# Gate and convolution projections of a hybrid decoder block: pairs of column blocks by seven block products in place of eight, gates parked in device memory

## The chip, the cores and the metric

One Trainium2 chip, one core. The metric is the device time of one execution in microseconds (us). All data are float32. A core has five engines with instruction queues of their own: TensorE (PE; loading its stationary operand is shown apart as PEld), VectorE (DVE), ScalarE (ACT), GpSimd (POOL) and SyncE (SP), whose queue here issues nearly all DMA transfers. Each queue is worked off in its order; an instruction that waits for a semaphore holds up those behind it.

## The reference

```python
h = rms_norm(x, norm_mix_g)                       # x: 1024 tokens x 1024
q, k, v, c_b, c_c, c_u, g_a, g_b = split(h @ w_in)  # 512 x 6 columns, then 1024 x 2
branch_a = stick_breaking_attention(q, k, v) @ w_sb_branch       # (512 -> 1024)
branch_b = short_conv_mixer(c_b, c_c, c_u, conv_w) @ w_conv_branch
merged = sigmoid(g_a) * branch_a + sigmoid(g_b) * branch_b
x = x + merged @ w_out
x = x + hierarchical_moe(rms_norm(x, norm_ffn_g))  # 32 experts, 2 per token
```

`short_conv_mixer` is c_b times a causal convolution of length 3, channel by channel, of c_c * c_u.

## The kernel before, in words

Every product is made from split operands: a float32 value is a high part (an fp32r copy, made on ACT) and a low part (value minus high part, made on DVE), and a product is three matmuls: high by high, high by low, low by high. In the projections the normalised, transposed input stands in SBUF as `hH` and `hL` (128 partitions x 8 k-blocks x 1024 tokens), a block of 128 weight columns is the stationary operand, and 512 tokens stream through.

The program has four stages. First (lines up to 570, put in order by a planner with costs, `Order`) come the norm, the projections q, k, v, the attention, and convolution block 0. Second, the stage that is edited, comes a plain list of jobs. Third are the output projection, second norm and routing, and fourth the experts, whose weights stream from memory.

A job makes one block of 128 output columns for 1024 tokens. `job_load` (L601 to L615) issues one DMA for the weights into one of two buffers `br`, and splits them into a third of `WH` and `WL` (three slots), ACT for the high part and DVE for the low one. `job_mm` (L617) does the matmuls, 48 with eight k-blocks and 24 with four, into two of the eight PSUM banks, and calls a closure that takes the result. The load of job n+2 is written ahead of the matmuls of job n.

The list has nine convolution jobs (blocks 1 to 3: c_c, c_u, c_b), then for each of eight merge blocks the gate g_b, its convolution branch, the gate g_a and its attention branch (the last two blocks are interleaved). `post_gb` and `post_ga` take a gate's sigmoid on ACT straight from PSUM, `post_bb` and `post_ba` multiply the branch by it on DVE, and POOL (DVE for the last two blocks) adds the two. The branches have k = 512. At the stage's start the attention output `attF` is split into `aH` and `aL`. In the last four jobs the blocks of w_out are loaded and split too (`out_w`).

Nothing plans this stage: each engine's order is that in which the code is written.

Of the kernel before, what the change touches and what calls it, by code (L numbers as in the profile page):

```python
# [21 lines left out]
F32 = mybir.dt.float32  # L22
# [8 lines left out]
N = 1024  # L31
# [67 lines left out]
def tile_hybrid_block(  # L99
# [481 lines left out]

    hlp = pool("hlp")
    aH = hlp.tile([128, 4, N], F32R, name="aH")
    aL = hlp.tile([128, 4, N], F32R, name="aL")
    c3 = hlp.tile([128, 2, 3, N], F32R, name="c3")
    v0 = VT0.rearrange("p t h d -> p (t h d)")
    cH = [v0[:, 0:N]] + [c3[:, 0, b] for b in range(3)]
    cL = [v0[:, N:2 * N]] + [c3[:, 1, b] for b in range(3)]
# [38 lines left out]
    hLk = [hL[:, k] for k in range(8)]  # L627
    aHk = [aH[:, k] for k in range(4)]
    aLk = [aL[:, k] for k in range(4)]

    cp = pool("cp", bufs=2)
    cst = {}

    def conv_jobs(b):
        def post_c(ps):
            cst["cc"] = cp.tile([128, N], F32, name="cc")
            S.activation(cst["cc"], ps, AF.Copy)

# [655 lines left out]
```

## Time and profile before

| | |
|---|---|
| time, three runs | median 1198.27 us (1198.21 to 1198.88) |
| the profiled execution | 1195.5 us, span 1193.7 us, mean granted clock 0.979 |
| PE, PEld busy | 1118.3 us (94%), 968.8 us (81%) |
| DVE, ACT, POOL busy | 761.7 us (64%), 656.8 us (55%), 343.2 us (29%) |
| the edited stage | 350.6 to 709.8 us |

The span runs from the first to the last instruction. Busy shares are means over stages with different limits; the rows below give the stage by itself. Instructions on one engine overlap a little, so that a busy time divided by a count is more than the distance from one start to the next.

### The profile page before, as it was taken

The page shows a single profiled execution, that of the slowest core. Times are in us where ns is not written, and L with a number is a line of the kernel's source. Part 1 is how long each engine was busy: PE and PEld are TensorE (multiplying, and loading weights), DVE is VectorE, ACT ScalarE, POOL GpSimd, SP SyncE. Part 2 cuts the span into 40 slices and gives each one's busy share as a digit, 9 for nine tenths or more (in the row PEclk, how much of TensorE's full clock was granted, in tenths as well). Part 3 has the DMA queues.
Part 4 walks back from the last instruction along what each step waited for, and adds up shares of the span by engine and source line. Part 5 has one row for each costly group of instructions (what it writes and reads, how often), then busy time and mean ns, then how long its engine had stood idle before and what let it go on. Part 6 is the DMA issues. An engine that isn't in the chain of part 4 may idle for free. (4 is left out here: it accounts for less than half of the span.)

```text
span 1193.7 us, 18153 instructions
## 1 busy us (share of the span) xinstructions
PE 1118.3 (94%) x6529; PEld 968.8 (81%) x6529; DVE 761.7 (64%) x1317; ACT 656.8 (55%) x1204; POOL 343.2 (29%) x661
## 2 busy tenths in 40 slices
PE   6999898998999999999999999899799999988894
PEld 5988797997788888888888888788588899977783
DVE  5579989989885332333233163444599998977683
ACT  6486768777654223222222132222489999977683
POOL 4636466363000000000000004545353223222121
PEclk9999999999999999999999999999899999999997
DMA  6000101001011111111112156837799999999992
GB/s 223 27 27 15 40 2 40 15 27 37 1 33 56 53 36 45 54 53 36 53 46 60 36 167 262 321 112 253 220 337 310 315 309 312 301 312 316 308 325 51
DMA packets 98323, 165.57 MB, mean 139 GB/s; under 512 B 13084, under 2 KB 62264, under 8 KB 98232
## 3 DMA queue, kind: packets, MB, share of 16 engines
q1 hardware_dynamic: 89016, 147.59, 36.8%
q0 software_dynamic: 9216, 16.81, 6.3%
q8 instruction: 52, 0.85, 0.3%
q14 instruction: 39, 0.32, 0.1%
HBM read 150.72 MB, written 19.92 MB: 143 GB/s over the span
## 5 line engine op out<-in xcount | busy, mean ns | idle before, releaser
L124 PE MATMUL PS<-WH,xet 128*88 128x256 f32 x768 | 153.2, 287 | 4.6 <-ACT sg L1159 4.6
L124 PE MATMUL PS<-hH,WH 128*128 128x512 f32 x448 | 143.9, 394 | 1.1 <-DVE attF L478 1.1
L124 PE MATMUL PS<-hH,WL 128*128 128x512 f32 x448 | 142.0, 390 | 0.0
L124 PE MATMUL PS<-hL,WH 128*128 128x512 f32 x448 | 141.9, 389 | 0.0
L124 PEld LDWEIGHTS PS<-WH,xet 128*88 128x88 f32 x768 | 109.5, 157 | 8.1 <-ACT sg L1159 5.4
L124 PE MATMUL PS<-WL,xet 128*88 128x256 f32 x384 | 109.2, 284 | 1.3 <-DVE WL L1103 1.2
L421 DVE TENSOR_TENSOR_SCAN pt<-pt 128x128 f32<-128x128 f32 (+2 forms) x96 | 93.4, 1013 | 16.3 <-issue 12.8
L674 POOL TENSOR_TENSOR mg<-mg,sga 128x1024 f32<-128x1024 f32 x6 | 14.7, 2455 | 293.0 <-DVE sga L672 293.0
L124 PEld LDWEIGHTS PS<-hH,WL 128*128 128x128 f32 x448 | 84.1, 188 | 17.6
L124 PEld LDWEIGHTS PS<-hH,WH 128*128 128x128 f32 x448 | 84.1, 188 | 17.5 <-ACT WH L610 1.2
L124 PEld LDWEIGHTS PS<-hL,WH 128*128 128x128 f32 x448 | 84.2, 188 | 16.4
L124 PE MATMUL PS<-WH,hH 128*128 128x384 f32 x256 | 91.8, 359 | 4.7 <-ACT hH L268 2.6
L611 DVE SCALAR_TENSOR_TENSOR WL<-br,cols,WH 128x128 fp32r<-128x128 f32 x200 | 68.9, 410 | 29.3 <-ACT WH L610 29.3
L124 PE MATMUL PS<-WH,hL 128*128 128x384 f32 x256 | 87.2, 340 | 0.1
L124 PE MATMUL PS<-WL,hH 128*128 128x384 f32 x256 | 86.7, 339 | 0.0
L615 DVE TENSOR_TENSOR WL<-br,WH 128x512 fp32r<-128x512 f32 x16 | 11.1, 691 | 116.5 <-ACT WH L614 116.5
L610 ACT ACTIVATE WH<-br,cols 128x128 fp32r<-128x128 f32 x200 | 65.4, 392 | 35.6 <-PE PS L124 34.4
L1092 POOL DMA_INDIRECT xr<-h2d,idx x32 | 45.3, 1414 | 78.7 <-PE PS L1134 69.5
L124 PE MATMUL PS<-WH,act 128*88 128x512 f32 x192 | 66.4, 400 | 1.2 <-ACT act L1168 1.2
L124 PEld LDWEIGHTS PS<-WL,xet 128*88 128x88 f32 x384 | 60.4, 157 | 4.6 <-DVE WL L1103 2.2
L124 PE MATMUL PS<-ahl,vt 128*128 128x256 f32 x320 | 53.5, 297 | 11.3 <-DVE attF L478 10.7
L460 POOL CAST ahl<-zeros 128x256 fp32r<-128x256 f32 x32 | 29.6, 934 | 115.3 <-PE PS L124 106.8
(278 smaller groups left out, 2735.1 us busy)
## 6 DMA issues: line engine op xcount, KB each, us to landing
br<-in_w_in_dram SPq DMA_DIRECT2D x25, 512.0 KB
cha<-in_w_gate_e_dram SPq DMA_DIRECT2D x22, 512.0 KB
cha<-in_w_up_e_dram SPq DMA_DIRECT2D x20, 512.0 KB
cha<-in_w_down_e_dram SPq DMA_DIRECT2D x18, 512.0 KB
mg<-in_w_down_e_dram SPq DMA_DIRECT2D x17, 512.0 KB
mg<-in_w_gate_e_dram SPq DMA_DIRECT2D x15, 512.0 KB
mg<-in_w_up_e_dram SPq DMA_DIRECT2D x14, 512.0 KB
br<-in_w_in_dram SPq DMA_DIRECT2D x36, 192.0 KB
```

The lines of the kernel that those rows point to most:

```text
L124: T.matmul(o, a, b, start=start, stop=stop)
L421: V.tensor_tensor_scan(pr, pr, pr, 1.0 if diag else P[:, j, w:w + 1], op0=OP.mult, op1=OP.bypass)
L460: G.tensor_copy(AHL[x][:, :, 0:128], zeros[:, None, :].to_broadcast([128, 2, 128]))
L610: S.activation(j.wH[:, k], r[:, k], AF.Copy, scale=g1[:, k:k + 1])
L611: V.scalar_tensor_tensor(j.wL[:, k], r[:, k], g1[:, k:k + 1], j.wH[:, k], op0=OP.mult, op1=OP.subtract)
L615: V.tensor_sub(j.wL[:, 0:nk], r[:, 0:nk], j.wH[:, 0:nk])
L674: (G if b < 6 else V).tensor_add(mg, mg, mst[b].rearrange("p (t c) -> p t c", c=128))
L1092: G.indirect_dma_start(out=XE[e % 2][:, :], out_offset=None, in_=h2d[:, :], in_offset=bass.IndirectOffsetOnAxis(ap=idx[0:SLOTS, EX[e]:EX[e ...
```

## The change

Two column blocks that are read from the same h make a pair. With K halved (k-blocks 0 to 3 and 4 to 7) and the tokens halved, a pair is a 2 x 2 by 2 x 2 block product, and it is made from seven block products of sums (a Strassen-Winograd scheme) in place of eight. There are eleven pairs: (c_c, c_u) of convolution blocks 2 and 3, (c_b of 2, c_b of 3), and (g_a, g_b) of each of the eight merge blocks. Convolution block 1 stays three plain jobs. A product is 4 k-blocks x 3 matmuls of 512 columns into one PSUM bank.

- `tprep` and `tprep4` make the four sums of h and split them, into `TT1`, `TT2`, `TT3` and, for the fourth, over a quarter of `hH` and `hL` that the plain jobs have read.
- `prep_op` multiplies the pair's weights by the norm's gain (DVE and POOL, once per pair), makes four sums of weights on POOL, and splits one operand per product into one of six slots; it runs five products ahead.
- `product` puts the seven results together on ACT and DVE. A finished gate is stored by SP into a tensor `gd` in device memory.
- After the last product come all eight attention branches and then all eight convolution branches. `gate_load` brings a gate back through SP into one of four buffers; the first four are issued ahead, and each later one behind the multiplication that uses the gate four before it.
- The attention output is split at the end of the products, the convolution result during the last attention branch. The blocks of w_out are loaded over more jobs than before.

The core of the diff (cut are the allocations, the plain jobs of block 1 and the closures of the convolution pairs, whose multiplications and taps run on DVE):

```diff
-    def job_mm(j, pair):
+    def job_mm(j, pair, mid=None):
         for k in range(j.nk):
             seq = ((j.wH, j.mH), (j.wH, j.mL), (j.wL, j.mH))
             for q, (w, m) in enumerate(seq):
                 for half in range(2):
                     mm(PS[:, 2 * pair + half, :], w[:, k], m[k][:, half * 512:(half + 1) * 512],
                        k == 0 and q == 0, k == j.nk - 1 and q == 2)
+        if mid:
+            mid()
         j.post(PS[:, 2 * pair:2 * pair + 2, :].rearrange("p b c -> p (b c)"))
...
+    def quad(K, tt):
+        return hH[:, K, tt], hL[:, K, tt]
+    B11, B12, B21, B22 = quad(K1, t1), quad(K1, t2_), quad(K2, t1), quad(K2, t2_)
...
+    TB4 = B12
+    def tprep(k):
+        a1, a2, a3, _ = [q.rearrange("p k c -> p (k c)") for q in SS]
+        def split(T, full):
+            S.activation(T[0][:, k], full, AF.Copy)
+            V.tensor_sub(T[1][:, k], full, T[0][:, k])
+        G.tensor_sub(a3, B22[0][:, k], B12[0][:, k])
+        G.tensor_add(a3, a3, B22[1][:, k])
+        G.tensor_sub(a3, a3, B12[1][:, k])
+        V.tensor_sub(a1, B12[0][:, k], B11[0][:, k])
+        V.tensor_add(a1, a1, B12[1][:, k])
+        V.tensor_sub(a1, a1, B11[1][:, k])
+        V.tensor_sub(a2, B22[0][:, k], a1)
+        V.tensor_add(a2, a2, B22[1][:, k])
+        split(TB1, a1)
+        split(TB2, a2)
+        split(TB3, a3)
...
+    def tprep4():
+        for k in range(4):
+            f = SGT[1][:, (t1, t2_)[k % 2]]
+            V.tensor_sub(f, B21[0][:, k], TB2[0][:, k])
+            V.tensor_add(f, f, B21[1][:, k])
+            V.tensor_sub(f, f, TB2[1][:, k])
+            S.activation(TB4[0][:, k], f, AF.Copy)
+            V.tensor_sub(TB4[1][:, k], f, TB4[0][:, k])
+    BOPS = [B11, TB2, B21, TB3, TB1, TB4, B22]
...
+    def g_post(b):
+        def post(q, ps, other):
+            blk, tt = q // 2, (t1, t2_)[q % 2]
+            sg = SGT[blk][:, tt]
+            V.tensor_add(sg, ps, other)
+            S.activation(sg, sg, AF.Sigmoid)
+            if q in (2, 1):
+                Y.dma_start(gd[8 * blk + b], SGT[blk])
+        return post
...
+    PAIRS = [(wcol(2048 + b * 128), wcol(2560 + b * 128), cu_post(b)) for b in (2, 3)]
+    PAIRS.append((wcol(1536 + 256), wcol(1536 + 384), b_post(2)))
+    PAIRS += [(wcol(3072 + b * 128), wcol(4096 + b * 128), g_post(b)) for b in range(8)]
...
+    def pair_load(g):
+        if g < len(PAIRS):
+            rw[g] = []
+            for src in PAIRS[g][0:2]:
+                r = brp.tile([128, 1024], F32, name="br").rearrange("p (k c) -> p k c", c=128)
+                Y.dma_start(r, src.rearrange("(k p) c -> p k c", p=128))
+                rw[g].append(r)
...
+    def prep_op(i):
+        if i >= NPR:
+            return
+        g, n = i // 7, i % 7
+        r1, r2 = rw[g]
+        if n == 0:
+            for E, r in ((V, r1), (G, r2)):
+                E.tensor_mul(r, r, g1[:, :, None].to_broadcast([128, 8, 128]))
+            G.tensor_add(SS[0], r2[:, K1], r2[:, K2])
+            G.tensor_sub(SS[1], SS[0], r1[:, K1])
+            G.tensor_sub(SS[2], r1[:, K1], r2[:, K1])
+            G.tensor_sub(SS[3], r1[:, K2], SS[1])
+        a = (r1[:, K1], SS[1], r1[:, K2], SS[2], SS[0], r2[:, K2], SS[3])[n]
+        s_ = slice(i % 6 * 512, i % 6 * 512 + 512)
+        wh, wl = [w[:, s_].rearrange("p (k c) -> p k c", c=128) for w in (WH, WL)]
+        S.activation(wh, a, AF.Copy)
+        V.tensor_sub(wl, a, wh)
+        if n == 6:
+            pair_load(g + 1)
+    def product(i):
+        g, n = i // 7, i % 7
+        o = PS[:, (i + 2) % 8, :]
+        s_ = slice(i % 6 * 512, i % 6 * 512 + 512)
+        wh, wl = [w[:, s_].rearrange("p (k c) -> p k c", c=128) for w in (WH, WL)]
+        bh, bl = BOPS[n]
+        for k in range(4):
+            mm3(o, wh[:, k], wl[:, k], bh[:, k], bl[:, k], k == 0, k == 3)
+        post = PAIRS[g][2]
+        if n == 0:
+            S.activation(P1, o, AF.Copy)
+        elif n == 1:
+            V.tensor_add(U2, o, P1)
+        elif n == 2:
+            post(0, o, P1)
+        elif n == 3:
+            V.tensor_add(U3, o, U2)
+        elif n == 4:
+            post(3, o, U3)
+            V.tensor_add(U2, o, U2)
+        elif n == 5:
+            post(2, o, U3)
+        else:
+            post(1, o, U2)
...
+    job_load(cj[0])
+    job_load(cj[1])
+    job_mm(cj[0], 3)
+    job_load(cj[2])
+    for k in (0, 1):
+        tprep(k)
+    job_mm(cj[1], 0)
+    for k in (2, 3):
+        tprep(k)
+    pair_load(0)
+    prep_op(0)
+    prep_op(1)
+    job_mm(cj[2], 3, tprep4)
+    for i in (2, 3, 4):
+        prep_op(i)
...
+    jobs = []
+    aH, aL = TT2, TT3
+    cH = [v0[:, 0:N]] + [aH[:, b] for b in range(3)]
+    cL = [v0[:, N:2 * N]] + [aL[:, b] for b in range(3)]
...
-    def conv_jobs(b):
-        def post_c(ps):
...
-    def merge_jobs(b):
...
-    for b in range(1, 4):
-        conv_jobs(b)
+    def gate_load(n):
+        if n < 16:
+            g = mst["mp"].tile([128, N], F32, name="gl")
+            Y.dma_start(g, gd[n])
+            mst[n] = g
+    def att_post(b):
+        def post(ps):
+            V.tensor_mul(MG[:, :, b, :], mst[b].rearrange("p (t c) -> p t c", c=128), ps.rearrange("p (t c) -> p t c", c=128))
+            gate_load(b + 4)
+        return post
+    def cnv_post(b):
+        def post(ps):
+            g = mst[8 + b]
+            V.tensor_mul(g, g, ps)
+            mg = MG[:, :, b, :]
+            (G if b < 5 else V).tensor_add(mg, mg, g.rearrange("p (t c) -> p t c", c=128))
+            gate_load(12 + b)
+        return post
...
     for b in range(8):
-        merge_jobs(b)
-    for js in mjobs[:6]:
-        for q in js:
-            job(*q)
-    for q in (0, 2, 1, 3):
-        for b in (6, 7):
-            job(*mjobs[b][q])
-    job_load(jobs[0])
-    job_load(jobs[1])
-    for p in range(4):
+        jobs.append(mkjob(w_sb_branch[0][:, b * 128:(b + 1) * 128], 4, False, aHk, aLk, att_post(b), b % 3))
+    for b in range(8):
+        jobs.append(mkjob(w_conv_branch[0][:, b * 128:(b + 1) * 128], 4, False, cH, cL, cnv_post(b), (8 + b) % 3))
...
+    def att_split(p):
         S.activation(aH[:, p], attF[0][:, p], AF.Copy)
         V.tensor_sub(aL[:, p], attF[0][:, p], aH[:, p])
...
+    for i in range(NPR):
+        product(i)
+        prep_op(i + 5)
+        if i == NPR - 3:
+            att_split(0)
+            att_split(1)
+            job_load(jobs[0])
+        elif i == NPR - 2:
+            att_split(2)
+            att_split(3)
+            job_load(jobs[1])
     attF[1].release()
+    stp.release()
+    mgp = pool("mgp", side="right")
+    MG = mgp.tile([128, 8, 8, 128], F32, name="mg")
+    mst["mp"] = pool("mp", side="right", bufs=4)
+    for n in range(4):
+        gate_load(n)
...
+    def cnv_split():
+        for b in range(3):
+            S.activation(aH[:, b], YC[b], AF.Copy)
+            V.tensor_sub(aL[:, b], YC[b], aH[:, b])
     for n, j in enumerate(jobs):
...
-        if left == 4:
+        if left == 12:
             out_tiles()
-            out_w(3)
-            out_w(4)
-        elif left == 3:
-            out_w(5)
-            out_w(6)
+        if left in (11, 10, 7, 6, 5):
+            out_w({11: 3, 10: 4, 7: 5, 6: 6, 5: 7}[left])
...
-        job_mm(j, (n - len(jobs)) % 4)
+        job_mm(j, n % 4, cnv_split if n == 7 else None)
```

How the order of instructions moves. The first place is DVE at the stage's start, with the weight splits of the plain jobs (`WL` from `br`). Before:

```order
L611 SCALAR_TENSOR_TENSOR WL_71<-br_3649,cols_110,WH_70 128x128 x8
L611 SCALAR_TENSOR_TENSOR WL_71<-br_3667,cols_110,WH_70 128x128 x8
L696 TENSOR_TENSOR aL_3644<-attF_580,aH_3643 128x1024 x4
L611 SCALAR_TENSOR_TENSOR WL_71<-br_3694,cols_110,WH_70 128x128 x8
L611 SCALAR_TENSOR_TENSOR WL_71<-br_3762,cols_110,WH_70 128x128 x8
L641 TENSOR_TENSOR cu_3828<-cc_3760,PS_65 128x1024
```

After, from the third job's weights to the first preparation's end (`ss0`, `ss1`, `ss2` are the sums, `tt1` to `tt3` their split; L655 to L659 depend on one another):

```order
L617 SCALAR_TENSOR_TENSOR WL_71<-br_3750,cols_110,WH_70 128x128 x8
L655 TENSOR_TENSOR ss0_3655<-hH_83 128x512
L656 TENSOR_TENSOR ss0_3655<-ss0_3655,hL_84 128x512
L657 TENSOR_TENSOR ss0_3655<-ss0_3655,hL_84 128x512
L658 TENSOR_TENSOR ss1_3656<-hH_83,ss0_3655 128x512
L659 TENSOR_TENSOR ss1_3656<-ss1_3656,hL_84 128x512
L650 TENSOR_TENSOR tt1_3654<-ss0_3655,tt1_3654 128x512
L650 TENSOR_TENSOR tt2_3643<-ss1_3656,tt2_3643 128x512
L650 TENSOR_TENSOR tt3_3644<-ss2_3657,tt3_3644 128x512
```

This group of eight stands there twice, then the multiplication and taps of the second job, the group twice more, gain and low parts of products 0 and 1, four groups for the fourth sum (three operations and a low part each), the multiplication of the third job, and only then the low part of product 2.

The second place is the SP queue in the branches (`br` is a weight load, `gd` the stored gates, `gl` a gate's buffer). Before, it held weight loads alone:

```order
L605 DMA br_4961<-in_w_sb_branch_dram 128x4x128
L605 DMA br_4990<-in_w_in_dram 128x8x128
L605 DMA br_5058<-in_w_conv_branch_dram 128x4x128
L605 DMA br_5088<-in_w_in_dram 128x8x128
L605 DMA br_5155<-in_w_sb_branch_dram 128x4x128
```

After, from the second branch job's weights on:

```order
L611 DMA br_5280<-in_w_sb_branch_dram 128x4x128
L704 DMA gd_3664<-sgt0_3662 128x1024
L811 DMA gl_5308<-gd_3664 128x1024
L811 DMA gl_5310<-gd_3664 128x1024
L811 DMA gl_5312<-gd_3664 128x1024
L811 DMA gl_5314<-gd_3664 128x1024
L611 DMA br_5316<-in_w_sb_branch_dram 128x4x128
L811 DMA gl_5345<-gd_3664 128x1024
L611 DMA br_5347<-in_w_sb_branch_dram 128x4x128
L811 DMA gl_5376<-gd_3664 128x1024
L611 DMA br_5378<-in_w_sb_branch_dram 128x4x128
```

The last store of a gate and four gate loads stand ahead of the third job's weights (`br_5316`). The load into `gl_5345` reuses the buffer of `gl_5308` and stands ahead of the fourth job's weights.

The third place is DVE in the same stretch (L615 and L621 are the low part of a job's weights, L665, L672 and L816 multiplications of a branch by its gate). Before:

```order
L672 TENSOR_TENSOR sga_5250<-sga_5250,PS_65 128x1024
L611 SCALAR_TENSOR_TENSOR WL_71<-br_5282,cols_110,WH_70 128x128 x8
L615 TENSOR_TENSOR WL_71<-br_5349,WH_70 128x512
L665 TENSOR_TENSOR mg_4308<-mg_4308,PS_65 128x8x128
L611 SCALAR_TENSOR_TENSOR WL_71<-br_5378,cols_110,WH_70 128x128 x8
```

After:

```order
L621 TENSOR_TENSOR WL_71<-br_5316,WH_70 128x512
L816 TENSOR_TENSOR mg_5304<-gl_5308,PS_65 128x8x128
L621 TENSOR_TENSOR WL_71<-br_5347,WH_70 128x512
L816 TENSOR_TENSOR mg_5304<-gl_5310,PS_65 128x8x128
L621 TENSOR_TENSOR WL_71<-br_5378,WH_70 128x512
```

Weights and multiplications alternate now with nothing between them.

## Rows read from the trace of the kernel before

**Rows 1.** The page, busy time, share of the span and instructions of each engine.
```profile
PE 1118.3 (94%) x6529; PEld 968.8 (81%) x6529; DVE 761.7 (64%) x1317; ACT 656.8 (55%) x1204; POOL 343.2 (29%) x661
```

**Rows 2.** Busy times by stretch: us, PE, PEld, DVE, ACT, POOL, clock, DMA, GB/s.
```profile
350.60:709.80 359.20, 359.11 (x1584) 297.41 (x1585) 129.53 (x265) 106.11 (x254) 14.73 (x6) 1.00 0.19 55
600.00:700.00 100.00, 100.00 (x443) 82.81 (x442) 26.75 (x54) 25.25 (x58) 4.88 (x2) 1.00 0.20 57
```

**Rows 3.** Timeline of ACT: start, duration, instruction, idle before it and its releaser.
```profile
655.63 1.03 ACT L661 ACTIVATE mg<-PS 128x1024 f32<-128x1024 f32 x1 [9.76 <-PE PS L124]
...
666.51 1.03 ACT L661 ACTIVATE mg<-PS 128x1024 f32<-128x1024 f32 x1 [7.52 <-PE PS L124]
```

**Rows 4.** Timeline of DVE, the first three jobs.
```profile
363.22 2.40 DVE L611 SCALAR_TENSOR_TENSOR WL<-br,cols,WH 128x128 fp32r<-128x128 f32 x8 [0.59 <-ACT WH L610]
372.75 1.22 DVE L641 TENSOR_TENSOR cu<-cc,PS 128x1024 f32<-128x1024 f32 x1 [7.13 <-PE PS L124]
374.01 0.75 DVE L372 TENSOR_SCALAR cc<-cu,cols 128x1024 f32<-128x1024 f32 x1
374.80 1.28 DVE L373 SCALAR_TENSOR_TENSOR cc<-cu,cols,cc 128x1023 f32<-128x1023 f32 x1
376.12 1.28 DVE L374 SCALAR_TENSOR_TENSOR cc<-cu,cols,cc 128x1022 f32<-128x1022 f32 x1
...
383.63 1.22 DVE L646 TENSOR_TENSOR cc<-cc,PS 128x1024 f32<-128x1024 f32 x1 [4.13 <-PE PS L124]
```

**Rows 5.** Groups by shape, 600 to 760 us: count, busy us, mean ns, idle before.
```profile
L867 POOL TENSOR_TENSOR hx<-xr,g 128x512 f32<-128x512 f32 x6 | 7.6, 1281 | 0.0
L674 POOL TENSOR_TENSOR mg<-mg,sga 128x1024 f32<-128x1024 f32 x2 | 4.9, 2439 | 60.4 <-DVE sga L672 60.4
L672 DVE TENSOR_TENSOR sga<-sga,PS 128x1024 f32<-128x1024 f32 x4 | 4.9, 1217 | 4.9 <-PE PS L124 4.9
L615 DVE TENSOR_TENSOR WL<-br,WH 128x512 fp32r<-128x512 f32 x6 | 4.1, 691 | 45.3 <-ACT WH L614 45.3
L614 ACT ACTIVATE WH<-br 128x512 fp32r<-128x512 f32 x6 | 3.7, 624 | 0.3 <-DMA br<-in_w_sb_branch_dram 0.3
L731 DVE TENSOR_TENSOR mhl<-mg,mhl 128x1024 fp32r<-128x1024 f32 x2 | 2.5, 1226 | 3.8 <-ACT mhl L730 3.8
```

**Rows 6.** Timelines of DVE and POOL, where both work at once.
```profile
253.69 2.46 DVE L421 TENSOR_TENSOR_SCAN pt<-pt 128x512 f32<-128x512 f32 x2 [0.63 <-ACT pt L405]
...
253.95 1.01 POOL L196 TENSOR_SCALAR nrA<-nrA 128x8 f32<-128x8 f32 x1
...
718.42 1.75 POOL L840 TENSOR_TENSOR wrt<-wrt,cols 128x288 f32<-128x288 f32 x1 [0.83 <-DMA wrt<-in_w_router_group_dram]
...
719.60 1.65 DVE L731 TENSOR_TENSOR vt<-mg,vt 128x1024 fp32r<-128x1024 f32 x1
```

**Rows 7.** Timelines of SP, two transfers issued, and of ACT, their first use.
```profile
690.63 0.34 SPq L714 DMA_DIRECT2D br<-in_w_out_dram  x1
691.83 0.38 SPq L605 DMA_DIRECT2D br<-in_w_sb_branch_dram  x1
...
694.09 1.15 ACT L724 ACTIVATE ow<-br 128x512 fp32r<-128x512 f32 x2 [3.18 <-DMA br<-in_w_out_dram]
695.60 0.63 ACT L614 ACTIVATE WH<-br 128x512 fp32r<-128x512 f32 x1 [0.35 <-DMA br<-in_w_sb_branch_dram]
...
718.63 0.90 SPq L805 DMA_DIRECT2D cha<-in_w_gate_e_dram  x2
```

**Rows 8.** Waits, 350 to 720 us: who for whom, us in total, times, longest.
```profile
ACT WH L614 <- DMA br<-in_w_sb_branch_dram: 0.3, 1, 0.3
```

**Rows 9.** Timeline of PE, then stretches as in rows 2, after an idle time.
```profile
849.80 1.40 PE L1134 MATMUL PS<-identF,xr 88*128 88x88 f32 x8 [5.04 <-DMA xr<-h2d,idx]
...
852.00:853.00 1.00, 1.00 (x6) 1.00 (x6) 0.26 (x1) 0.00 (x0) 0.57 (x1) 0.50 1.01 348
853.00:854.00 1.00, 1.00 (x9) 1.00 (x8) 0.00 (x0) 0.09 (x1) 0.00 (x0) 0.80 1.02 336
```

More of the change, by code (lines that the diff above doesn't have):

```diff
@@ L582, in tile_hybrid_block, with mkjob @@
     hlp = pool("hlp")
-    aH = hlp.tile([128, 4, N], F32R, name="aH")
-    aL = hlp.tile([128, 4, N], F32R, name="aL")
-    c3 = hlp.tile([128, 2, 3, N], F32R, name="c3")
+    TT2 = hlp.tile([128, 4, N], F32R, name="tt2")
+    TT3 = hlp.tile([128, 4, N], F32R, name="tt3")
+    yp = pool("yp")
+    YC = [yp.tile([128, N], F32, name=f"yc{b}") for b in range(1, 4)]
+    stp = pool("stp")
+    TT1 = stp.tile([128, 4, N], F32R, name="tt1")
+    SS = [stp.tile([128, 4, 128], F32, name=f"ss{i}") for i in range(4)]
+    P1, U2, U3 = [stp.tile([128, 512], F32, name=f"pu{i}") for i in range(3)]
+    SGT = [stp.tile([128, N], F32, name=f"sgt{i}") for i in range(2)]
+    gd = dram.tile([16, 128, N], F32, name="gd")
     v0 = VT0.rearrange("p t h d -> p (t h d)")
-    cH = [v0[:, 0:N]] + [c3[:, 0, b] for b in range(3)]
-    cL = [v0[:, N:2 * N]] + [c3[:, 1, b] for b in range(3)]
+    t1, t2_ = slice(0, 512), slice(512, 1024)
+    K1, K2 = slice(0, 4), slice(4, 8)
     class Job:
         pass
-    jobs = []
-    def job(src, nk, gain, mH, mL, post):
+    def mkjob(src, nk, gain, mH, mL, post, slot):
         j = Job()
-        j.src, j.nk, j.gain, j.mH, j.mL, j.post = src, nk, gain, mH, mL, post
-        j.slot = len(jobs) % 3
-        jobs.append(j)
+        j.src, j.nk, j.gain, j.mH, j.mL, j.post, j.slot = src, nk, gain, mH, mL, post, slot
+        return j
     def job_load(j):
@@ new lines, in tprep4, with cu_post @@
+    def tprep4():
[7 more added lines that the diff above has]
+    BOPS = [B11, TB2, B21, TB3, TB1, TB4, B22]
+    def cu_post(b):
+        y, cu = YC[b - 1], SGT[0]
+        def post(q, ps, other):
+            blk, tt = q // 2, (t1, t2_)[q % 2]
+            V.tensor_add((y, cu)[blk][:, tt], ps, other)
+            if q in (2, 1):
+                V.tensor_mul(cu[:, tt], cu[:, tt], y[:, tt])
+            if q == 1:
+                conv_taps(V, y, cu, b)
+        return post
@@ new lines, in b_post, with post @@
+    def b_post(b0):
+        def post(q, ps, other):
+            blk, tt = q // 2, (t1, t2_)[q % 2]
+            y, sg = YC[b0 - 1 + blk][:, tt], SGT[blk][:, tt]
+            V.tensor_add(sg, ps, other)
+            V.tensor_mul(y, y, sg)
+        return post
+    def g_post(b):
+        def post(q, ps, other):
+            blk, tt = q // 2, (t1, t2_)[q % 2]
+            sg = SGT[blk][:, tt]
+            V.tensor_add(sg, ps, other)
+            S.activation(sg, sg, AF.Sigmoid)
+            if q in (2, 1):
+                Y.dma_start(gd[8 * blk + b], SGT[blk])
+        return post
@@ new lines, in tile_hybrid_block, with post_c, post_u, post_b @@
+    cj = []
+    def post_c(ps):
+        S.activation(YC[0], ps, AF.Copy)
+    def post_u(ps):
+        V.tensor_mul(SGT[0], YC[0], ps)
+        conv_taps(V, YC[0], SGT[0], 1)
+    def post_b(ps):
+        V.tensor_mul(YC[0], YC[0], ps)
+    for n, (base, post) in enumerate(((2048, post_c), (2560, post_u), (1536, post_b))):
+        cj.append(mkjob(wcol(base + 128), 8, True, hHk, hLk, post, n))
+    job_load(cj[0])
[4 more added lines that the diff above has]
+        tprep(k)
@@ L765, in tile_hybrid_block @@
     mst["mp"].release()
+    yp.release()
     hlp.release()
```

52 lines of the change are left out of this document (8 added, 44 removed).

## The prediction, made before the changed kernel had run

> **What bounds the kernel now.** I read the page's busy table first, then the busy times by stage, the timeline of the stage that is edited, the groups by shape, and the SP queue. TensorE is busy for 94% of the span [rows 1]; the stage from 350.6 to 709.8 us (nine convolution, sixteen gate and sixteen branch products) has 359.11 us of PE work in 359.20 us at granted clock 1.00, while DVE is busy for 129.5, ACT for 106.1 and POOL for 14.7 us [rows 2]. It is a pure stream: ACT picks up one finished gate job at 655.63 and the next at 666.51, 10.88 us for 48 matmuls of 512 columns, 0.2267 us each [rows 3]; 1584 of them make 359.1 us. The reader should see that only the PE counts here, so a matmul removed is worth its time in full, but only as long as operands arrive faster than every 2.72 us (12 matmuls) in the products and every 5.44 us (24) in the branches. That condition is where I look.
>
> **Removed.** Of 25 jobs of 48 matmuls, 22 become 11 pairs of 7 products of 12: 1200 fall to 3 x 48 + 924 = 1068. 132 x 0.2267 = 29.9 us less PE work.
>
> **Added at the start: the sums of h.** The third plain job has its low parts ready on DVE at 365.6 (363.22 + 2.40) [rows 4], and PE has work until 383.3, just before DVE picks that third job up [rows 4]. In front of the third product's weights DVE's row now has (the order of DVE, above): four preparations, each five dependent 512-column operations and three low parts, the latter waiting for copies on ACT. With 0.69 us per DVE and 0.62 per ACT operation [rows 5], 0.04 between dependent operations (as between the taps [rows 4]) and 0.60 between independent ones, one is 5 x 0.73 + 3 x 0.60 + 0.1 = 5.6 us, four 22.4. The second job's multiply and taps: 4.7 (372.75 to 377.4) [rows 4]. Gain and two low parts with their ACT copies: 4.4. The fourth sum: per k three dependent operations, an ACT copy, a low part, 3.5, four 14.0. The third job's multiply and the wanted low part: 1.9. Together 47.4: the third product could start at 413.0.
>
> POOL works beside this: nine more 512-column operations at 1.28 us, four at the start of the first pair, a 1024-wide gain at 2.44 [rows 5]; 19.1 us. Do they run beside DVE? The rows say no. A DVE subtraction of two SBUF tiles that takes 1.23 us elsewhere [rows 5] took 1.65 from 719.60, and ended 1.08 after POOL's multiply of 718.42 + 1.75 = 720.17; and a POOL operation on 8 columns took 1.01 us beside DVE's scans, ending as the first of them did [rows 6]. So they exclude each other. The chain grows by 0 to 19.1; I take 15, since about a fifth falls into DVE's own waits: third product at 428. The Trainium skill says the same ("SBUF — State Buffer", section "Who interferes with whom": a DVE instruction with two SBUF inputs contends with a GpSimd one that reads SBUF, and the loser waits for the whole instruction); the trace agrees, and by the opposite view, free sharing, the start would be 15 us earlier.
>
> PE does products 0 and 1 in that gap. PE that idled 5.04 us before 849.80 ran at clock 0.50 from 852 to 853 and at 0.80 over the next microsecond, so at half until about 853.4 [rows 9]: 3.6 us at half speed, 1.8 us lost. The other 898 matmuls take 203.6. Last product at 428 + 1.8 + 203.6 = 633.4 at the earliest.
>
> **The pairs.** PE needs 19.04 us per pair; DVE has about 11 us, ACT 7.4, POOL 2.44 + 4 x 1.28 = 7.6, so busy time fits. The chain per pair may not: the second half's weights are loaded again only after five more low parts; three of those rounds are add, sigmoid, copy, low part (2.5 us each) and two are short, 8.7; the load 3.5 alone [rows 7] or 5.5 behind two gate stores; gain and two sums on POOL 5.2; copy and low part 1.3: 18.7 to 20.7 us, and up to 2.6 more for the shared access. Against 19.04 this costs -0.3 to 4.3 per pair, once the lead of five us is used up. Bounds 0 and 30; I take 10, two us on five pairs: last product ends at 643.4.
>
> **The branches.** Before, the SP queue there held only weight loads, and the branch weights were late once, by 0.3 us [rows 8]. Now gate loads stand in it. Each, from the fifth on, reuses a buffer, so SP waits at it for the DVE multiply that reads the old gate, and behind it in the same queue stands the load of a later job's weights (the order of SP, above). DVE's row in turn has those weights' low part ahead of the next multiply (the order of DVE, above). This closes a ring: multiply 1.22 [rows 5], semaphore 0.1, gate load and weights, ACT copy 0.67, low part 0.65. The trace has such a pair of transfers: 512 KB issued at 690.63, 256 KB at 691.83, used at 694.09 and 695.60, 4.97 us after the first issue [rows 7]. One round is 7.6 us, and PE needs 5.44. If the small load does not queue behind the big one (0.45 later [rows 7] plus its own 3.77) it is 6.85, still more.
>
> The start is worse. DVE's row after product 74 is two adds, two 1.22 us splits of the attention output, the first branch weights, the add of product 75, two splits, the second branch weights, the add of product 76. Counted from the end of product 74: 5.5 to the first weights, 1.3 for add and sigmoid, 5.0 for the gate store that this sigmoid releases and the weight load behind it, 1.4 for copy and low part, 1.5 for the last add and sigmoid: 14.7, which is 9.3 after product 76. Then come one store, four gates and the third job's weights. Six transfers at 1.6 to 2.4 us (I take 2.1, and 1.5 for the small one, with 1.5 before the first) and a copy: the third job starts 23.5 us after the last product, not 10.9.
>
> From there, by rounds: five at 7.6; two that also bring w_out blocks (2.7 more for a transfer and two low parts) 10.3; one with the convolution split (three 1.14 us subtractions and a copy) 11.5; one with POOL's add of 2.44 before the gate's buffer is free, 10.1; three with that add and a w_out block, 12.8. Sum 118.6 to the fifteenth job's weights; the last two jobs 10.9, the clock 1.8. In all 23.5 + 118.6 + 12.7 = 154.8 where PE has 87.1 of work. Out-projection then starts at 643.4 + 154.8 = 798.2 instead of 709.8, and everything after is unchanged code behind it: +88.4 us.
>
> The Trainium skill's fit for one transfer ("DMA: Bandwidth & Descriptors", "Anatomy of one DMA — SWDGE (gpsimd) path") is 2.0 us + bytes/436 GB/s, for the POOL path: 3.8 us for the 768 KB of a round, an estimate, where the row has 4.97 on SP's. By it a round is 6.4 and the total some 14 us less.
>
> **Sum.** The profiled execution took 1195.5 us (span 1193.7), the median is 1198.27. 1195.5 + 88.4 = 1283.9; on the median, 1286.7, so 1287 us.
>
> **Rivals.**
> A, the forecast: 1287, own range 1268 to 1308.
> B, the same rings, but DVE and POOL share freely and transfers are quick: -15 at the start, -10 in the pairs, -3.5 at the third job, -0.75 on 12 rounds = -9: +51, 1249. For it: POOL's 512-column multiplies have a steady mean of 1.28 us [rows 5], whatever DVE does. Against it: [rows 6, 7].
> C, the pair ring at its upper bound (+20), slower gate transfers (+5), the port in full (+4): +117, 1316.
> D, the gate loads hold nothing up and the branches run at PE's pace. With the shared access +23 (428 + 205.4 + 10 + 2.5 + 87.1 = 733), 1221; without it, and without loss in the pairs, 413 + 205.4 + 0.7 + 87.1 = 706.2, -3.6, 1195. For it: ACT and DVE stand idle for about two thirds of the stage now [rows 2]. Against it: the ring needs no busy engine, only latencies, and decides as soon as a round exceeds 5.44 us.
> E, all of the sums hidden: -29.9, 1168. It would need the fourth sum not to stand in DVE's row ahead of the third product's low part.
>
> **How the numbers follow.** A 0.57, B 0.17, C 0.08, D with the port 0.06, D without 0.07, E 0.05. Slower: A, B, C and the first D, 0.88. Faster by over 0.2% (2.4 us, about what a measurement of this kernel tells from none): E and most of the last D, 0.10; same 0.02. The range 1240 to 1315 holds A, B and most of C.
>
> **What would show it.** Right: PE idle from 383 to about 405 and again for some 10 us before the third product; gaps of 1 to 3 us at pair boundaries late in the stage; a gap of about 11 us before the third branch job, then one before each; SP waiting at the gate loads for DVE, and ACT for the branch weights, 60 us together; PE idle for some 115 us between 350 and the out-projection. Wrong: branch jobs 5.44 us apart (D), or the third product before 415 (B). After the out-projection starts, stages as long as before; if they differ by over 5 us, the sum is wrong there.

## The result, and the profile after

The changed kernel takes 1259.86 us (1259.34 to 1261.07) where the kernel before takes 1198.58: ratio 1.052, interval 1.0505 to 1.0535. Slower, as forecast; 27 us less than the 1287 forecast. The profiled execution took 1259.34 us.

Busy times by stretch after the change, with the columns of [rows 2]: up to product 0, to product 2 (to its third matmul, which waited for the low part; the first two ran from 422.55), to the end of the products, to the third branch job, to the output projection, and the rest:

```profile
351.00:404.73 53.73, 32.89 (x145) 26.93 (x145) 43.93 (x62) 15.34 (x37) 19.56 (x12) 0.85 0.10 30
404.73:424.49 19.76, 9.35 (x27) 6.28 (x27) 16.31 (x21) 5.67 (x11) 4.02 (x3) 0.67 0.00 0
424.49:634.71 210.22, 207.99 (x898) 170.12 (x899) 129.65 (x176) 66.15 (x115) 76.86 (x50) 0.99 0.28 87
634.71:653.83 19.12, 11.60 (x49) 8.67 (x47) 4.51 (x7) 4.43 (x6) 0.00 (x0) 0.95 0.55 192
653.83:773.91 120.08, 91.40 (x336) 70.59 (x337) 43.17 (x48) 20.55 (x32) 12.87 (x9) 0.84 0.37 115
773.91:1257.00 483.09, 437.90 (x2913) 379.47 (x2911) 333.96 (x526) 306.74 (x438) 166.63 (x281) 0.96 0.84 272
```

The stage is 422.9 us long, before 359.2 [rows 2], although its 1452 matmuls are only 329.2 us of work at 0.2267. Behind it nothing changed: 483.7 us to the end of the span (1257.6 - 773.91), before 483.9 (1193.7 - 709.8). The first two rows hold 170 matmuls (38.5 us) in 73.5 us, the last two of the stage 384 (87.1 us) in 139.2; the products between them run nearly at PE's pace (898 matmuls, 203.6 us, in 210.2). PE's timeline names what it waited for:

```profile
404.73 0.79 PE L124 MATMUL PS<-hH,WH 128*128 128x512 f32 x1 [20.84 <-ACT WH L739]
...
422.55 0.79 PE L124 MATMUL PS<-hH,WH 128*128 128x512 f32 x1 [9.65 <-ACT WH L739]
...
424.49 0.80 PE L124 MATMUL PS<-hH,WL 128*128 128x512 f32 x1 [0.72 <-DVE WL L740]
...
653.83 2.07 PE L124 MATMUL PS<-tt,WH 128*128 128x512 f32 x4 [7.10 <-ACT WH L620]
```

The ring of the branches, one turn of it: SP, ACT and DVE.

```profile
669.92 0.32 SPq L811 DMA_DIRECT2D gl<-gd  x1
670.33 0.39 SPq L611 DMA_DIRECT2D br<-in_w_sb_branch_dram  x1
...
676.54 0.32 SPq L811 DMA_DIRECT2D gl<-gd  x1
```
```profile
674.02 0.63 ACT L620 ACTIVATE WH<-br 128x512 fp32r<-128x512 f32 x1 [5.99 <-DMA br<-in_w_sb_branch_dram]
```
```profile
668.68 1.21 DVE L816 TENSOR_TENSOR mg<-gl,PS 128x1024 f32<-128x1024 f32 x1
674.69 0.69 DVE L621 TENSOR_TENSOR WL<-br,WH 128x512 fp32r<-128x512 f32 x1 [4.79 <-ACT WH L620]
675.30 1.21 DVE L816 TENSOR_TENSOR mg<-gl,PS 128x1024 f32<-128x1024 f32 x1
```

DVE's multiplication ends at 669.89, SP issues the gate load 0.03 us later and the weights behind it, ACT has them at 674.02, DVE's low part and then the next multiplication follow: 6.62 us from one to the next, PE needs 5.44. The ring is made of waits and not of work: DVE is busy for 43.17 of the 120.08 us, ACT for 20.55. Waits of DVE and ACT from 350 to 800 us and of SP from 350 to 774 (us in total, times, longest):

```profile
DVE WL L621 <- ACT WH L620: 83.6, 14, 11.5
ACT WH L620 <- DMA br<-in_w_conv_branch_dram: 54.9, 7, 9.9
ACT WH L620 <- DMA br<-in_w_sb_branch_dram: 37.8, 6, 10.2
SPq L811 <- DVE mg L816: 55.9, 8, 9.5
SPq L811 <- POOL mg L825: 39.5, 4, 10.5
```

SP stood at the gate loads (L811) for DVE's multiplications, and in the last rounds for POOL's additions.

### The profile page after: what moved, and what is told of

Its sections match the earlier page's. It is cut to its first block, busy times and chain, and to the rows that moved or that the text cites. A ratio compares the mean times of both kernels' runs of the same rounds, so it can differ in the third digit from the quotient of the medians.

```text
span 1257.6 us, 18033 instructions
## 1 busy us (share of the span) xinstructions
PE 1111.8 (88%) x6397; PEld 952.4 (76%) x6397; DVE 863.6 (69%) x1359; ACT 661.4 (53%) x1146; POOL 445.1 (35%) x727
## 5 line engine op out<-in xcount | busy, mean ns | idle before, releaser
L124 PE MATMUL PS<-tt,WH 128*128 128x512 f32 x488 | 149.4, 407 | 19.5 <-ACT WH L620 10.8
L124 PE MATMUL PS<-hH,WH 128*128 128x512 f32 x272 | 106.2, 405 | 31.6 <-ACT WH L739 30.5
L124 PEld LDWEIGHTS PS<-tt,WH 128*128 128x128 f32 x488 | 95.3, 197 | 45.1 <-ACT WH L620 13.3
L124 PE MATMUL PS<-hH,WL 128*128 128x512 f32 x272 | 104.2, 397 | 0.8 <-DVE WL L740 0.7
L124 PE MATMUL PS<-hL,WH 128*128 128x512 f32 x272 | 103.7, 396 | 0.0
L124 PE MATMUL PS<-tt,WL 128*128 128x512 f32 x244 | 88.8, 402 | 1.2 <-DVE WL L740 1.2
L124 PE MATMUL PS<-WH,hL 128*128 128x384 f32 x256 | 87.1, 340 | 0.0
L124 PEld LDWEIGHTS PS<-hH,WH 128*128 128x128 f32 x272 | 52.1, 192 | 41.9 <-ACT WH L739 31.3
L740 DVE TENSOR_TENSOR WL<-ss,WH 128x512 fp32r<-128x512 f32 x44 | 35.1, 800 | 57.5 <-ACT WH L739 57.4
L1245 POOL DMA_INDIRECT xr<-h2d,idx x32 | 41.5, 1296 | 81.9 <-PE PS L1287 80.4
L731 POOL TENSOR_TENSOR br<-br,cols 128x1024 f32<-128x1024 f32 x11 | 22.9, 2084 | 132.6 <-DMA br<-in_w_in_dram 119.6
L621 DVE TENSOR_TENSOR WL<-br,WH 128x512 fp32r<-128x512 f32 x16 | 11.0, 690 | 83.6 <-ACT WH L620 83.6
## 6 DMA issues: line engine op xcount, KB each, us to landing
mg<-in_w_down_e_dram SPq DMA_DIRECT2D x17, 512.0 KB, 12.7
```

Of the source, the lines that this page charges most:

```text
L124: T.matmul(o, a, b, start=start, stop=stop)
L621: V.tensor_sub(j.wL[:, 0:nk], r[:, 0:nk], j.wH[:, 0:nk])
L731: E.tensor_mul(r, r, g1[:, :, None].to_broadcast([128, 8, 128]))
L740: V.tensor_sub(wl, a, wh)
L1245: G.indirect_dma_start(out=XE[e % 2][:, :], out_offset=None, in_=h2d[:, :], in_offset=bass.IndirectOffsetOnAxis(ap=idx[0:SLOTS, EX[e]:EX[e ...
```

## The experiments

Stage lengths here run from the stage's first matmul (it starts between 349.4 and 352.6 us) to the first of the output projection: 359.1 us before, 422.9 in the changed kernel. They come from the one profiled execution of each kernel. A ratio sets a kernel's median against that of the kernel before, timed beside it (1194.65 to 1198.58 us).

**The branches' ring.** In r1_loads_first the gate load moves behind the next weight load:

```diff
         def post(ps):
             V.tensor_mul(MG[:, :, b, :], ...)
-            gate_load(b + 4)
...
             job_load(jobs[n + 2])
+        if n > 0:
+            gate_load(n + 3)
```

> Edit: each later gate load stands behind the next job's weight load in SP's queue, not ahead of it; all else as in the changed kernel. Ring theory (the weight load waits in SP's queue behind a gate load that waits for DVE's multiplication, and that multiplication waits in DVE's queue behind earlier weights): the ring now spans two jobs, 7.6 us for two, so the branch jobs go at PE's 5.44 us, or some 6 where w_out blocks load too. Third job at about 654 us as in the changed kernel, then 14 jobs in 76 to 82 us instead of 120: output projection at about 735 (773.9 in the changed kernel), time about 1221 us. Rival, transfers: the same 16 gate loads and as many bytes still pass through SP and the DMA engines, so rounds stay at 6.6 to 12 us and the time at 1250 to 1260. Rival, clock: PE is slow because it idled; it then speeds up only as far as the gaps go, which this run does not tell from the ring.

In r2_six_buffers the order stays and the wait goes:

```diff
-    mst["mp"] = pool("mp", side="right", bufs=4)
+    mst["mp"] = pool("mp", side="right", bufs=6)
```

> Edit: six gate buffers in place of four, the order of all queues as in the changed kernel. The gate loaded behind multiplication n now goes into the buffer of gate n-2, long free, so SP no longer waits for DVE there, but every weight load still stands behind a 512 KB gate load. Ring theory: the wait was the cost, so as with the order changed: output projection at about 735, time about 1221 us. Rival, the 512 KB ahead of each weight load is the cost (its transfer, not the wait): 1240 to 1260.

Measured: r1 1229.32 us, ratio 1.030 (1.026 to 1.034), stage 393.3; r2 1218.27, ratio 1.020 (1.018 to 1.023), stage 381.8. r2 loads the same bytes in the same order, so the wait was the price, not the transfers. PE in r2 from the third job's weights to the output projection is full:

```profile
653.70:732.91 79.21, 79.19 (x336) 65.25 (x337) 45.41 (x50) 21.04 (x32) 14.51 (x9) 0.96 0.52 167
```

r1 missed its 1221 us by 8, and its SP and DVE rows say why: the first attention jobs did run at 5.44, but where a w_out block is loaded, that load now stands behind the waiting gate load, and its low parts on DVE ahead of the next multiplication. The ring had only passed to the next transfer in the queue, at 10.9 us a turn:

```profile
712.48 0.33 SPq L811 DMA_DIRECT2D gl<-gd  x1
712.92 0.36 SPq L870 DMA_DIRECT2D br<-in_w_out_dram  x1
...
723.39 0.33 SPq L811 DMA_DIRECT2D gl<-gd  x1
```
```profile
718.10 1.29 DVE L882 TENSOR_TENSOR ow<-br,ow 128x512 fp32r<-128x512 f32 x2 [7.90 <-ACT ow L880]
719.31 1.22 DVE L822 TENSOR_TENSOR gl<-gl,PS 128x1024 f32<-128x1024 f32 x1
```

**The third branch job.** b1_six_third_first is r2 with one load moved ahead of the first gates:

```diff
+    job_load(jobs[2])
     for n in range(4):
         gate_load(n)
```

> Edit: six gate buffers, as in r2_six_buffers, and the third branch job's weight load issued ahead of the first four gate loads. If the third job's start (19.1 us after the last product, of which 8 idle) comes from the 2 MB of gates ahead of its weights, the idle time shrinks to 1 to 2 us and with it the half clock behind it: 5 to 8 us less than r2_six_buffers, 1210 to 1213 us. If it comes from DVE's and ACT's queues (the splits of the attention output), the time stays at 1218.

Measured: 1216.21 us, ratio 1.017 (1.013 to 1.020), above the 1210 to 1213 expected; the stage is 378.0 us, 3.8 less than in r2, while the intervals of the two ratios overlap. The third job's wait fell from 6.9 us in r2 to 0.7, but the fourth job's weights now stood behind the gates:

```profile
648.14 1.19 PE L124 MATMUL PS<-tt,WH 128*128 128x512 f32 x4 [0.73 <-ACT WH L620]
...
657.27 2.07 PE L124 MATMUL PS<-tt,WH 128*128 128x512 f32 x4 [3.38 <-ACT WH L620]
```

**The start, and the pairs.** h1_sum4_later moves the fourth sum behind the weights of products 2 to 4:

```diff
-    job_mm(cj[2], 3, tprep4)
+    job_mm(cj[2], 3)
     for i in (2, 3, 4):
         prep_op(i)
+    tprep4()
```

> Edit: the fourth sum of h (16 DVE operations, 14 us) is written behind the weights of products 2, 3 and 4 in place of ahead of them; it is needed by product 5 alone. DVE chain theory: product 2 starts at about 409.5 us in place of 424.5, products 2 to 4 run beside the fourth sum, and product 5 follows at the sum's pace, done some 10 to 11 us earlier than in the changed kernel: time about 1249 us. Rival, the pairs' ring (weights of the next pair) sets the pace of what follows and takes the gain back: 1255 to 1260.

Measured: 1258.51 us, ratio 1.054 (1.051 to 1.057), stage 420.8. The start did what was expected: product 5 started at 423.17, where the changed kernel was at product 2 (424.49). The rival won: 2 us are left in the stage, and none that the ratios tell. In the gate pairs PE's waits recur every 20 us, and PE is busy for 97.3 of 101 us:

```profile
534.60 0.50 PE L124 MATMUL PS<-tt,WL 128*128 128x512 f32 x1 [0.40 <-DVE WL L740]
...
554.67 0.50 PE L124 MATMUL PS<-tt,WL 128*128 128x512 f32 x1 [0.40 <-DVE WL L740]
```
```profile
530.00:631.00 101.00, 97.32 (x417) 77.38 (x417) 58.27 (x79) 36.81 (x63) 36.42 (x24) 1.00 0.30 97
```

ACT's copies of the gate pairs' first products lie 20.4 us apart in h1 (499.86 to 622.18, six pairs) and 20.3 in the changed kernel (503.71 to 625.34): the ring was there as well, hidden by the lead of the weights until PE's first wait at 577.69, in the ninth pair. h3_sum4_later_pair_loads has h1's edit, and loads each weight block of the next pair as soon as its own buffer is read:

```diff
-        if n == 6:
-            pair_load(g + 1)
+        if n in (2, 5):
+            pair_load(g + 1, (0 if n == 2 else 1,))
```

> Edit: the fourth sum later, as in h1_sum4_later, and the two weight blocks of the next pair loaded each as soon as its own buffer is read (after the third and the sixth operand of a pair) in place of both after the seventh. Pairs' ring theory (in h1_sum4_later product 5 started 11 us earlier, but the pairs then took 20.4 us each in place of 19.04 and gave most of it back, because the next pair's sums waited for their load): the ring shrinks by one product and by the load that queued ahead, 3 us or more, so pairs take 19.04 us each, the 11 us stay, the third branch job starts at about 643 us in place of 650 (h1) and 654 (the changed kernel), time 1247 to 1251 us. Rival, the lead is lost elsewhere (POOL's own work, DVE's queue): the third job stays at 650, time 1258.

Measured: 1254.03 us, ratio 1.048 (1.045 to 1.051), stage 415.6; gate pairs 19.2 us apart (501.75 to 617.14), third job 293.5 us into the stage (changed kernel 302.8). In h1 the third job came after 300.8 us, so 7.3 us of the lead had gone into the ring that these loads close. PE no longer waits in the gate pairs:

```profile
530.00:628.00 98.00, 98.00 (x434) 81.14 (x433) 55.51 (x79) 37.43 (x65) 35.28 (x24) 1.00 0.29 100
```

In the three convolution pairs it still does, 0.6 us at 445.60 and at 465.99, where h1 waits 0.6 at 443.65 and 464.03: those waits are not the loads', and what causes them was not tested. The time came out 3 us above the range: of the 9.3 us by which the third job came earlier than in the changed kernel, 2.0 were lost behind it, in the branches' ring.

In h2_pool_sums_out POOL has less to do beside DVE, since the third sum of h is left out:

```diff
-        G.tensor_sub(a3, B22[0][:, k], B12[0][:, k])
-        G.tensor_add(a3, a3, B22[1][:, k])
-        G.tensor_sub(a3, a3, B12[1][:, k])
...
-        split(TB3, a3)
+        split(TB3, B22[0][:, k])
```

> Edit: the third sum of h, three POOL operations per k-block, is left out (the high part of one block of h is split in its place, so the output is not the reference's). DVE's queue is unchanged. Shared access theory: in the changed kernel DVE operations beside POOL's nine at the start took 1.6 to 2.2 us in place of 0.7 to 1.3, about 7.5 us together; they shrink to the durations alone, product 2 starts at about 417 in place of 424.5, time about 1252 us. Rival, free sharing (DVE's long ones have another cause, such as PSUM reads or ACT beside it): no change, 1260.

Measured: 1256.07 us, ratio 1.052 (1.049 to 1.054): in time no more than the measurement can tell. In the trace product 2 starts 65.9 us into the stage (418.50, stage from 352.62) in place of 73.5, 7.6 us earlier (7.5 expected); at the output projection 3.4 are left, the rest was lost behind it. DVE's operations beside POOL's nine in the changed kernel add up to the same: each took 0.9 to 1.0 us more than in h2, eight of them 7.6 us. DVE beside POOL in the changed kernel, and the same sum in h2:

```profile
371.39 0.69 DVE L655 TENSOR_TENSOR ss<-hH 128x512 f32<-128x512 f32 x1
372.11 1.66 DVE L656 TENSOR_TENSOR ss<-ss,hL 128x512 f32<-128x512 f32 x1
373.80 1.66 DVE L657 TENSOR_TENSOR ss<-ss,hL 128x512 f32<-128x512 f32 x1
375.50 1.67 DVE L658 TENSOR_TENSOR ss<-hH,ss 128x512 f32<-128x512 f32 x1
...
379.91 1.22 DVE L776 TENSOR_TENSOR sgt<-yc,PS 128x1024 f32<-128x1024 f32 x1
```
```profile
371.55 1.67 POOL L652 TENSOR_TENSOR ss<-hH 128x512 f32<-128x512 f32 x1 [25.44 <-DVE tt L650]
373.30 1.62 POOL L653 TENSOR_TENSOR ss<-ss,hL 128x512 f32<-128x512 f32 x1
374.99 1.62 POOL L654 TENSOR_TENSOR ss<-ss,hL 128x512 f32<-128x512 f32 x1
379.96 1.30 POOL L652 TENSOR_TENSOR ss<-hH 128x512 f32<-128x512 f32 x1 [3.35 <-DVE tt L650]
```
```profile
375.22 0.69 DVE L653 TENSOR_TENSOR ss<-ss,hL 128x512 f32<-128x512 f32 x1
375.94 0.69 DVE L654 TENSOR_TENSOR ss<-ss,hL 128x512 f32<-128x512 f32 x1
376.67 0.69 DVE L655 TENSOR_TENSOR ss<-hH,ss 128x512 f32<-128x512 f32 x1
```

**A version that beats both.** With six buffers, the third job first and the loads of h3, the start is left. Plain jobs cost 2.72 us more per pair replaced and give PE 21.8 us of work ahead of product 0:

```diff
+    for b in range(2):      # f5: range(1)
+        for blk in range(2):
+            cj.append(mkjob(wcol(3072 + 1024 * blk + b * 128), 8, True, ..., plain_gate(blk, b), 0))
...
+    for i in range(4):
+        prep_op(i)
+    job_mm(cj[-1], 3)
+    prep_op(4)
+    tprep4()
```

> Edit: all three rings opened (six gate buffers, third job first, pair loads each at its own time), and seven plain jobs at the start in place of three: the gates of merge blocks 0 and 1 are made plainly, nine pairs in place of eleven, and the sums of h stand in DVE's queue between the plain jobs, the fourth behind the weights of products 0 to 4. 1476 matmuls in the stage, 334.6 us, 5.4 us more than the changed kernel; PE has 43.5 us more work ahead of product 0, which covers DVE's chain of some 50 us. If the three places are the whole loss, the stage takes 338 to 345 us in place of 423, and the time is 1178 to 1186 us, under the kernel before. If other losses stand behind them, 1195 or more.

> Edit: as f7_seven_plain, but only merge block 0's gates made plainly: five plain jobs, ten pairs, 1464 matmuls, 331.9 us. PE runs out of plain work at about 405 us, DVE has product 0's weights at about 410: an idle time of 4 to 6 us, half clock behind it, and product 5 some 4 us late. Stage 342 to 350 us, time 1181 to 1190 us: slower than seven plain jobs by 0 to 6 us although it has 2.7 us less work, if DVE's chain at the start is what the plain jobs hide.

Measured: f7_seven_plain 1200.09 us, ratio 1.003 (1.002 to 1.005); f5_five_plain 1193.54, 0.998 (0.996 to 1.000). Both missed. In f7_seven_plain a branch job's weights are written into a slot that the last product still has to read: PE waited 8.5 us there, and that product uses the wrong weights, so the output is not the reference's. In f5_five_plain no product's weights are overwritten, and PE's long waits are 3.8 us before product 0 and 4.4 before product 5. The next two shift the slots and load the gates two ahead:

```diff
-    jobs.append(mkjob(..., att_post(b), b % 3))
+    jobs.append(mkjob(..., att_post(b), (b + 2) % 3))
```

> Edit: as f7_seven_plain, with the branch jobs' weight slots shifted by two thirds (in f7_seven_plain and f5_five_plain a branch job's weights were written into a slot that one of the last products still had to read, so those two products read the wrong weights and waited for their load), and the gates loaded two ahead in place of four, so that the fourth job's weights have fewer gates ahead of them in SP's queue. If the start's chain, the pairs' ring and the branches' ring are the whole loss, 1476 matmuls (334.6 us) and 4 to 9 us of remaining idle time: the stage takes 339 to 344 us in place of 359.2 before, ratio to the kernel before 0.983 to 0.990. If the start is covered but the time is not, over 0.995.

> Edit: as f7_slots with five plain jobs and ten pairs: 1464 matmuls, 331.9 us, 2.7 us less work, but some 10 us of idle time and half clock at the start that seven plain jobs hide (in f5_five_plain PE idled 3.8 us before product 0 and 4 us before product 5): stage 345 to 350 us, ratio 0.988 to 0.994. Faster than f7_slots only if the start's chain costs less than 2.7 us.

Measured: f7_slots 1197.37 us, ratio 1.0005 (0.999 to 1.002), stage 360.5 (339 to 344 expected); f5_slots 1189.90, 0.994 (0.992 to 0.997), stage 353.2 (353.4 in f5_five_plain, so the slots were not its loss), 3 us above the range. Against the expectation seven plain jobs lost to five. PE's two long waits in f7_slots have causes besides the start's chain:

```profile
451.10 0.79 PE L124 MATMUL PS<-hH,WH 128*128 128x512 f32 x1 [6.24 <-ACT WH L739]
...
621.92 2.04 PE L124 MATMUL PS<-tt,WH 128*128 128x512 f32 x4 [7.14 <-DVE sgt L701]
```

The second is PSUM: with 63 products the first branch job gets the last product's bank, and the add that frees it stands behind the splits in DVE's queue. The first is SP's queue once more: a gate's store waits for its sigmoid, and the weights of the next plain jobs and of the first pair stand behind it, so that DVE's chain starts late.

```profile
397.78 0.34 SPq L787 DMA_DIRECT2D gd<-sgt  x1
398.21 0.39 SPq L611 DMA_DIRECT2D br<-in_w_in_dram  x1
412.46 0.34 SPq L787 DMA_DIRECT2D gd<-sgt  x1
412.90 0.39 SPq L611 DMA_DIRECT2D br<-in_w_in_dram  x1
420.97 0.34 SPq L787 DMA_DIRECT2D gd<-sgt  x1
421.40 1.42 SPq L721 DMA_DIRECT2D br<-in_w_in_dram  x2
```

f5_order took the other way, more product work beside DVE's chain:

```diff
+    FIRST = (0, 2, 6, 1, 3, 4, 5)      # order of the first pair's products
```

> Edit: as f5_slots, and the first pair's products in the order 1, 3, 7, 2, 4, 5, 6: the three that need no sum of h come first, their weights are prepared ahead of the last k-block's sums in DVE's queue (the temporaries of those sums moved to other tiles), and the seventh's result stays in PSUM until the others are there. In f5_slots PE idled about 4 us before the first product, about 4 us before the product of the fourth sum, and ran at half clock behind both. If DVE's chain at the start is the loss, 8.2 us of product work now lie beside it: the idle time before the first product goes, 2 to 3 us stay before the fourth sum's, and the stage shrinks from 353 to 343 to 347 us: ratio 0.985 to 0.991. If the loss is in the pairs behind it, no change: 0.994.

Measured: 1193.93 us, ratio 0.998 (0.997 to 0.999), slower than f5_slots, where 0.985 to 0.991 was expected. The wait before product 0 went, and the one before the fourth sum's product grew from 4.1 to 7.9 us:

```profile
433.00 0.79 PE L124 MATMUL PS<-hH,WH 128*128 128x512 f32 x1 [7.88 <-ACT WH L743]
```

The fourth sum's product starts 81.1 us into the stage, in f5_slots 79.3: DVE's chain ends no earlier for what PE does in between, and products moved forward only bring the wait together. f7_banks frees the loads and the bank:

```diff
         if n + 2 < NP:
             job_load(cj[n + 2])
+        else:
+            pair_load(0)
         job_mm(cj[n], (3, 0)[n % 2])
...
-        job_mm(j, n % 4, ...)
+        job_mm(j, (1, 0, 2, 3)[n % 4] if n < 4 else n % 4, ...)
```

> Edit: as f7_slots, with three things that its profile shows: the plain jobs' weight loads (and the first pair's) are written one job earlier, ahead of the store of a gate (in f7_slots they stood behind it in SP's queue, the last plain job's weights came 1.3 us late, the first pair's gain on DVE waited until 425.8 and the fourth sum until 436.9, so PE idled 6.2 us before product 5); and the first two branch jobs swap their PSUM banks (in f7_slots the first one had the bank of the last product, whose add stood behind the splits of the attention output in DVE's queue: 7.1 us idle). If these are the losses: 9 us of idle time and some 6 us of half clock go, the stage falls from 361 to 343 to 349 us, ratio 0.986 to 0.992. If seven plain jobs lose elsewhere: 0.995 or more.

Measured: 1183.90 us (1182.16 to 1187.40), ratio 0.990 (0.988 to 0.992), stage 349.5. It beats both kernels, by 1% the kernel before. The waits that were 6.2 and 7.1 us in f7_slots are down to

```profile
443.93 0.50 PE L124 MATMUL PS<-hH,WH 128*128 128x512 f32 x1 [2.86 <-ACT WH L739]
...
616.70 1.15 PE L124 MATMUL PS<-tt,WH 128*128 128x512 f32 x4 [1.23 <-DVE sgt L701]
```

and the first is the longest in the stage. Of the 349.5 us 334.6 are matmul work at 0.2267; for 8.6 PE is idle (3.9 between 430 and 470 us, 3.3 between 610 and 640), and its matmuls take 6.3 more. The causes of these were not taken apart further. The profiled execution, 1187.40 us, was the longest of the six.

## Why the prediction was right, point by point

- **The range**: 1259.86 us lies within 1240 to 1315, but below A's own 1268 to 1308, and nearer to B's 1249 than to A's 1287. The mechanism is A's: the rings hold PE up (r2, h3), and DVE and POOL do not share freely (h2). B was right that transfers are quicker than the rows said. All terms behind the first erred the same way, so nothing cancelled.
- **Removed**: 29.9 us, right; the matmul count fell by 132.
- **The start**: product 2 forecast at 428, measured 424.5. The chain without POOL was 413.0 by the sum; sharing added some 11.5 us, not 15. By their durations, DVE's operations beside POOL took 12.7 us more up to there than alone (0.69 us for 512 columns, 1.28 for a tap); h2 shows that 7.6 of them are POOL's third sums, so POOL's share in the loss is shown. Rival B's free sharing is not what happened.
- **The pairs**: forecast 18.7 to 20.7 us a turn and 10 us lost; the turn measured 20.3 and the loss 6.6 (210.2 for 203.6, of which some 2 at granted clock 0.50 from 422.55 to 428.50). The ring was right (h1 and h3 show it), but the lead of five products lasted through eight pairs, and PE's waits at the last three were 0.4 to 0.6 us each, not 1 to 3.
- **The third branch job**: forecast 23.5 us after the last product, measured 19.1. The store left SP 8.25 us after the last product (642.96 - 634.71; forecast 9.3), and from there the store, four gates and weights took 10.2 us, not 13.5: six transfers overlap more than 2.1 us each allows.
- **The rounds**: the ring is what was forecast (r2), its size was not. Twelve rounds took 107.7 us, forecast 118.6: the attention rounds 6.6 to 6.8 after a first 7.7, where 7.6 was taken for all; by the spacing of SP's gate loads the later ones took 9.0 and 9.2 for 10.3, 10.4 for 11.5, 9.3 for 10.1 and 11.5 to 12.2 for 12.8. The mis-sized term is the pair of transfers, from the gate load's issue to ACT's use of the weights: 4.97 us from [rows 7], here 4.1 to 4.3 in ten of the rounds (669.92 to 674.02 above) and 5.2 and 5.5 in the others, some 7 of the 10.9 us; the rest was not taken apart. The attention rounds are nearest to the lower value, 6.85, where the small load does not queue behind the big one. The Trainium skill's fit ("DMA: Bandwidth & Descriptors", section "Anatomy of one DMA — SWDGE (gpsimd) path"), which is for POOL's path, gave an estimate of 3.8 us for the two transfers and of 6.4 a round; what most rounds took lies between it and the row.
- **Sum**: the terms were too long by 3.5, 5.2, 4.4 and 10.9 us, and 0.3 in the last two jobs: 24.3, which takes the 1283.9 for the profiled execution to 1259.6, measured 1259.34.
- **What would show it**: PE idle for some 115 us was forecast; 93.7 (422.9 - 329.2) were lost, 69.7 of them idle and 24.0 as slower matmuls, most of them (15.2) in the rounds, at granted clock 0.84. The forecast had 3.6 for the clock. SP's and ACT's waits, forecast as 60 us together, were larger: SP 55.9 for DVE and 39.5 for POOL, ACT 92.7.

## What to carry to other kernels

A change that takes work from the bounding engine is worth it only as far as the operands keep up: look for rings of latencies (queue order, a buffer's reuse, a semaphore) whose turn is longer than the bounding engine's new period, since no busy share shows them. A transfer that waits for a compute engine must not stand in a queue ahead of loads that the same engine's next step needs; two more buffers (r2: 41 us) opened the ring where a new order only passed it on (r1). A gain at one place counts only when the next ring behind it is open too: h1, b1 and f5_order each moved the loss.

## What the runs showed of the hardware

- DVE and POOL, each with its operands in SBUF, nearly take turns: three DVE and three POOL operations of 512 columns took 5.62 us (371.55 to 377.17), where one after the other they are 5.91 (3 x 0.69 + 3 x 1.28) and side by side 3.84. The DVE multiplication at 379.91 that reads one operand from PSUM kept its 1.22 us beside POOL's 1.30. The Trainium skill ("SBUF — State Buffer", section "Who interferes with whom") says that a DVE instruction with two SBUF inputs contends with a GpSimd one that reads SBUF, and that one with at most one SBUF input does not, outside the two-port modes. These rows agree.
- Four gate loads and a weight load (2.25 MB) were issued from 643.37 on and used at 653.15: 9.8 us. One 512 KB load took 3.46 us from issue to use in the kernel before (690.63 to 694.09, [rows 7]), so the five overlap.
